# One-hot rows of a routing-weight table: made in bfloat16 by the vector engine, eight tokens at a time

## The chip, the core and the metric

The kernel runs on one core of a Trainium2 chip. The core has a matrix engine (TensorE, in the profile PE for its products and PEld for its weight loads), a vector engine (VectorE, DVE), a scalar engine (ScalarE, ACT), GpSimd (POOL) and SyncE (SP), which here only issues transfers. Every engine works through its own list of instructions in a fixed order and waits on semaphores for the others. The metric is the device time of one execution in microseconds (us), the median of the runs.

## The reference

Two layers of a diffusion transformer: 512 latent tokens and 256 context tokens of 1024 channels. Each layer has three mixers, a merge and, at its end, a retrieval of experts with product keys. Only the last matters here, cut to its core (per token block):

```python
s1, i1 = lax.top_k(s[:, :, 0], 16)            # 8 heads, two halves of 128 keys each
s2, i2 = lax.top_k(s[:, :, 1], 16)
cand_s = (s1[..., :, None] + s2[..., None, :])
top_s, pos = lax.top_k(cand_s, 16)            # the 16 best pairs: expert i1*128 + i2
g = softmax(top_s)
act = gelu(einsum('td,thkd->thk', t, u_tab[idx]))
return einsum('thk,thkd->td', g * act, v_tab[idx])
```

There are 128 x 128 = 16384 experts and each token uses 8 x 16 = 128 of them.

## The kernel before

Everything is done in float32 precision. Large products split each operand into a high part with few significant bits and an exact rest (`split`, lines 96 to 109: ACT makes the high part on line 102, DVE or POOL subtracts it on line 109) and add three products (`mm3`, lines 113 to 115). "alt" as an engine means that DVE and POOL take the subtraction in turns.

The experts are evaluated in two ways. A few token blocks of 128 tokens gather the rows of their experts from DRAM, one expert row of every token at a time (`step`, line 838 on POOL asks for the rows, lines 857 and 866 on DVE use them); these steps are spread over the whole program. For the other latent blocks, four in layer 0 and three in layer 1 (`NDBS`), all 16384 experts are evaluated densely, 128 experts (a chunk) at a time: `dense_u` makes gelu(u h) for a chunk, 24 products, tile du, then gS; `dense_v` multiplies gS by the routing weights of the chunk and multiplies by v (tiles da and d).

The routing weights must stand as a dense table [i1][i2][token] in DRAM before `dense_v` can start. `gtable` makes it, one block of 128 tokens at a time, for seven blocks or 896 tokens in all. A block is transposed on PE so that the 128 (head, rank) slots lie on the partitions (i1, i2 and the weight g of each slot; line 896), and ACT copies these to the tile sT (lines 899, 900, the second negated). Then, for each token, two matrices of 128 slots x 128 columns are made: oa, with a one where the column is i1, and ob, with g where the column is i2. One product per token of ob and oa (line 919, tile px) sums over the slots and gives the token's 128 x 128 table. In detail, for four tokens at a time:

- oa: one DVE instruction, a comparison of 512 float32 elements (line 908).
- ob: one instruction per token, and the engine depends on the token: the letters of `OB = ("PADD", "AADD")` are POOL, ACT and DVE. So of eight tokens POOL makes one and DVE four, each in one instruction (line 916), and ACT three, each in two instructions (lines 913, 914).
- four products on PE in float32; the trace records two matrix instructions for each (1792 for 896 tokens).
- one ACT copy of 512 elements from PSUM to the staging tile stg (line 920). After 16 tokens SP stores stg in DRAM (line 921), and `gtable` yields.

oa and ob have three buffers each (`OBB`), px has two PSUM banks.

The work around it: `layer` interleaves four generators, among them `routing` (norm, `route1`, then `route2` for each block), `table` (`gtable` for each dense block once its `route2` is done) and `fill`, which runs `dense_u` ahead of the table. `route2` picks the 16 best pairs on DVE (lines 684 to 688) and looks up their keys: a DVE comparison of 2048 bfloat16 elements into a tile oh (line 773, its first operand a broadcast with an innermost step of 0), a POOL product in place (line 776), a DVE sum (line 777). The pool gives this tile, tag "oh", one buffer. `fill` keeps the results of its chunks in buffers: `NGSS = (16, 30)` of them in SBUF for layers 0 and 1, besides 40 chunks per layer that go to DRAM. The remaining chunks of u are made in the dense stage, between the v parts. The order in which each engine finally runs its instructions is fixed when the program is built, by a planner with its own durations; products of du stand between products of px in it.

Of the kernel before, what the change touches and what calls it, by code (L numbers as in the profile page):

```python
# [10 lines left out]
F32 = mybir.dt.float32  # L11
F32R = mybir.dt.float32r
# [9 lines left out]
P = 128  # L22
# [8 lines left out]
CAND = 112         # pairs of best keys that can be among the 16 best  # L31
NK = 128
NDBS = (4, 3)      # latent token blocks whose experts are evaluated densely, per layer
OBB = 3            # buffers of the one-hot rows
XB = 2             # steps of adaLN before each of the first two norms
XA = (4, 4)        # and before the loads of each of the inputs
GP = ("px", "px")  # PSUM tags of the routing-weight table
BRE = "dve"        # engines: split of the mixers' results,
YS = "dve"         # split of the merged mixers,
ADDE = "dve"       # sums of the mixers  # L40
OB = ("PADD", "AADD") # engines of the one-hot rows of four tokens, in turns
PQB = (2, 2)       # buffers of the query weights of the routing: split, and as loaded
PQC = None         # and of the context
US = ("alt", "alt") # engine that splits the expert tables beside the routing, per layer
GT = 16            # tokens per group of the routing-weight table
NCG = 8            # chunks of experts per read of that table
TILE = 1800        # ns to load a weight tile
STEPS = ((1700, 1700, 1700), (1700, 1700, 1700)) # ns between two steps of the gathered experts: mixers, dense experts
LAG = 3            # steps from a gathered product to its sum
NGSS = (16, 30)    # chunks of experts by which u runs ahead of v, per layer  # L50
SPILL = ((40, 3), (40, 3)) # chunks whose u part goes to DRAM early, one in so many, per layer
FILL = (1.0, 1.3)  # steps of u and adaLN per step of the routing
LEAD = 2           # of which so many after the routing
ADA = 6            # adaLN column groups of the next layer beside its predecessor's routing
WBUFS = ((3, 2), (3, 4)) # buffers of weight tiles: split, and as loaded, per layer
FB = (1, 2)        # buffers of the Fourier matrices, per layer
PE2 = ("alt", "dve") # engines that split the weights of the projections, per layer
PE3 = ("dve", "dve") # and of q, k and v
ME = ("alt", "pool") # engines that split the weights of the merge beside the attention, per layer
CR = 1.75          # steps of the routing of the context per step of the last merge  # L60
CR2 = 1            # and per step of the routing of the latents
GATES = (0.5, 0.6) # steps of the gates per step of the Fourier and chunk mixers, per layer
ATT = (3, 1)       # steps of the merge per step of the attention, per layer
AN = (0.1, 0.2)    # and per step of the second norm
AD = (0.25, 0.3)   # steps of adaLN per step of the Fourier and chunk mixers, per layer

# tile numbers of the packed projection weights
# [6 lines left out]
PBANKS = {"ps": 4, "px": 2, "tl": 1, "fl": 1}     # PSUM banks of the projections  # L74
RBANKS = {"ps": 3, "px": 2, "tl": 2, "fl": 1}     # and from the attention on


class Ker:
# [19 lines left out]
    def split(self, H, L, src, h="act", l="dve"):  # L98
        """src = H + L, H with float32r's significant bits, L the exact rest."""
        nc = self.nc  # L100
        if h == "act":
            nc.scalar.activation(H, src, AF.Copy)  # L102
        else:
            nc.vector.tensor_copy(H, src)
        if l == "alt":          # both in turns
            self.turn = not self.turn
            l = "dve" if self.turn else "pool"
        e = nc.vector if l == "dve" else nc.gpsimd
        e.tensor_tensor(L, src, H.bitcast(F32), op=ALU.subtract)  # L109
# [8 lines left out]
    def mm3pair(self, out, qH, qL, kH, kL, h, qs):  # L118
        """the two halves of a head's 128 rows, on the two row tiles of the array."""
# [6 lines left out]
    def hilo(self, src, l="dve", own=None):  # L126
        """a [128, 1024] weight tile from DRAM, in two float32r parts; own: (pool, buffers of the parts, and as loaded)."""
# [17 lines left out]
    def interleave(*threads, until=None):  # L145
        """emits generators in turns, each (generator, steps per turn); all, or until one ends."""
# [19 lines left out]
    def rstd(self, tmp, r, v, scale, shape, tag, bufs=1, eps=None):  # L166
        """r = (v * scale + eps) ** -0.5: Newton steps from the guess that halves the exponent."""
# [16 lines left out]
    def setup(self):  # L184
# [9 lines left out]
        self.csil = cp.tile([P, KD, 4], F32R, name="csilr")      # high parts of both vectors, then low parts  # L194
# [13 lines left out]
    def setup_rest(self):  # L208
# [3 lines left out]
        self.iota = cp.tile([P, P], F32, name="iota")  # L212
        nc.sync.dma_start(self.iota, a["iota"])
        self.iota16 = cp.tile([P, TOPK], BF16, name="iota16")
        nc.vector.tensor_copy(self.iota16, self.iota[:, :TOPK])
        for l, v in enumerate(self.lay):
# [11 lines left out]
            nc.vector.tensor_tensor(v["lam"], e[:, 1:2], e[:, 0:1], op=ALU.subtract)     # minus lambda  # L228
# [4 lines left out]
    def ada(self, l, ccs, pool=None, e="dve", tag="tl"):  # L233
        nc = self.nc
        sm, mod = self.lay[l]["sm"], self.lay[l]["mod"]
        for cc in ccs:
# [19 lines left out]
            if cc in (3, 9):          # norm gain times (1 + scale)  # L256
# [7 lines left out]
    def sumsq(self, tmp, S, k, src, tag="nt", bufs=2):  # L264
        """adds the squares of channel block k to S."""
# [8 lines left out]
    def rms(self, tmp, S, scale, T, ps=None):  # L274
        """1 / rms of the columns of S (squares, summed over the partitions), on every partition, in PSUM."""
        return self.spread(self.rmsd(tmp, S, scale, T, ps), T, ps)

    def rmsd(self, tmp, S, scale, T, ps=None, eps=None):
        """its first half: the values as diagonal matrices of 128 columns each."""
# [17 lines left out]
    def stat(self, tmp, r, T, load):  # L297
        """r = 1 / rms of the columns."""
# [4 lines left out]
    def norm(self, tmp, l, xd, T, which, si, outs, r=None, x=None, *_):  # L303
        """outs(k) -> (H, L) for channel block k; xd: [128, 8, T] in DRAM; r: 1 / rms where known; x: xd in SBUF."""
# [23 lines left out]
    def projT(self, l, n, ss, e="pool", tag=None, own=None):  # L328
        """(h @ W)^T of each stream: 128 columns on the partitions."""
# [10 lines left out]
    def projN(self, l, n, ss, e="pool"):  # L340
        """h @ W for 512 columns of each stream, tokens on the partitions."""
# [14 lines left out]
    def qknorm(self, tmp, accs, g, rope, oH, oL):  # L356
        """accs: PSUM [128 tokens, 512]; oH, oL: [128 (m, dim), head, token]."""
# [58 lines left out]
    def softmax(self, tmp, l, h, q0, qH, qL, T, klat, kctx, ze):  # L416
        """the two softmaxes of a head for 256 queries and their difference, per 128 queries; ze: EPS for the norm."""
# [13 lines left out]
        for qb in range(2):  # L431
# [18 lines left out]
            # the difference, times the sum of the first softmax, which the norm of the result takes out again  # L450
# [941 lines left out]
```

## Time and profile before

| | us |
|---|---|
| median of 3 runs | 5004.7 (4994.27 to 5005.57) |
| span of the profiled execution | 4993.1 |
| PE busy | 4532.1 |
| DVE busy | 3535.6 |
| POOL busy | 2083.6 |
| ACT busy | 1995.8 |

The span runs from the first to the last instruction of one profiled execution. It is 1.2 us below the fastest of the runs and 11.6 us below their median. Busy time counts the time in which an engine had an instruction in work; for DVE and POOL that includes time in which the instruction was held up, as some rows below show. The table stage of layer 0 lies at 1280 to 1680 us and that of layer 1 at 3840 to 4130 us; what comes before is the mixers and most of the routing, and what comes after each is the dense stage.

### The profile page before, as it was taken

The numbers are of one execution on the slowest core, as the hardware profiler recorded it, in microseconds if no ns is written. First come the engines' busy times: TensorE is split into PE (matmuls) and PEld (weight loads), VectorE is DVE, ScalarE is ACT, GpSimd is POOL, SyncE is SP. The second block draws the span as 40 slices with busy tenths as digits, with TensorE's granted clock in tenths as the row PEclk, the third lists the DMA queues.
The fourth block names the chain that finished last, engine by engine and source line by source line (L and its number), as shares of the span: only waits on it lengthen the run. The fifth ranks groups of instructions, "written<-read, shape, count | busy, mean of one in ns | idle before, by whom it ended". The sixth has DMA issues, their size and how long they took to land.

```text
span 4993.1 us, 64879 instructions
## 1 busy us (share of the span) xinstructions
PE 4532.1 (91%) x23117; PEld 3852.4 (77%) x23117; DVE 3535.6 (71%) x6922; ACT 1995.8 (40%) x3274; POOL 2083.6 (42%) x1262
## 2 busy tenths in 40 slices
PE   7999989788788899999999989989897899999998
PEld 4887778667566688877778767767687788999998
DVE  6335585977998677766767875457559986777787
ACT  4433443232678522222222233334333783333332
POOL 2111013345656565655556421111326665555531
PEclk8999999899999999999999989999898999999999
DMA  4532345566566889988889876233535668888886
GB/s 167 178 115 65 98 128 180 165 191 197 193 232 226 290 288 318 320 281 270 280 284 304 310 256 217 94 102 110 163 97 180 214 245 293 294 293 301 300 286 232
DMA packets 447364, 1092.82 MB, mean 219 GB/s; under 512 B 37056, under 2 KB 193600, under 8 KB 439872
## 3 DMA queue, kind: packets, MB, share of 16 engines
q1 hardware_dynamic: 336448, 685.97, 42.4%
q0 software_dynamic: 110592, 402.70, 23.7%
q8 instruction: 182, 2.98, 0.2%
q14 instruction: 142, 1.16, 0.1%
HBM read 970.04 MB, written 118.49 MB: 218 GB/s over the span
## 4 chain that ended last, share of the span: by engine, by line
PE 55%; DVE 17%; issue 8%; DMA 8%; POOL 5%; ACT 3%; SPq 0%; POOLq 0%; ACTq 0%; DVEq 0%
PE du L113 6%; PE du L115 5%; PE du L114 5%; PE da L114 5%; PE da L113 5%; PE da L115 5%; PE ps L114 3%; PE ps L113 3%; PE ps L115 3%; DVE row L857 2%; POOL row L838 2%; DMA row<-in_u_dram,idxc 2%; PE px L919 2%; POOL wL L109 2%; DVE wL L109 2%
## 5 line engine op out<-in xcount | busy, mean ns | idle before, releaser
L109 POOL TENSOR_TENSOR wL<-wraw,wH 128x1024 fp32r<-128x1024 f32 x307 | 761.7, 2482 | 1197.1 <-ACT wH L102 1066.9
L102 ACT ACTIVATE wH<-wraw 128x1024 fp32r<-128x1024 f32 x556 | 586.8, 1058 | 1231.5 <-PE du L114 337.2
L113 PE MATMUL du<-dH,wH 128*128 128x512 f32 (+1 forms) x2048 | 779.9, 381 | 64.4 <-DVE da L980 46.3
L115 PE MATMUL du<-dH,wL 128*128 128x512 f32 (+1 forms) x2048 | 773.2, 378 | 49.0 <-POOL wL L109 27.4
L114 PE MATMUL du<-dL,wH 128*128 128x512 f32 (+1 forms) x2048 | 770.2, 376 | 4.1 <-DVE dL L325 4.1
L114 PE MATMUL da<-AL,vH 128*128 128x512 f32 (+1 forms) x1792 | 650.5, 363 | 3.0 <-DVE AL L109 2.9
L113 PE MATMUL da<-AH,vH 128*128 128x512 f32 (+1 forms) x1792 | 646.4, 363 | 6.0 <-ACT AH L102 6.0
L115 PE MATMUL da<-AH,vL 128*128 128x512 f32 (+1 forms) x1792 | 649.5, 362 | 0.0
L857 DVE SCALAR_TENSOR_TENSOR row<-row,hn 128x1024 f32<-128x1024 f32 x384 | 526.9, 1392 | 99.4 <-DMA row<-in_u_dram,idxc 83.6
L102 ACT ACTIVATE vH<-vr 128x1024 fp32r<-128x1024 f32 x256 | 271.7, 1062 | 772.5 <-PE da L114 559.3
L109 DVE TENSOR_TENSOR wL<-wraw,wH 128x1024 fp32r<-128x1024 f32 x249 | 336.9, 1355 | 330.7 <-ACT wH L102 316.7
L866 DVE SCALAR_TENSOR_TENSOR acc<-row,dots,acc 128x1024 f32<-128x1024 f32 x381 | 502.9, 1320 | 10.8 <-DMA row<-in_v_dram,idxc 6.9
L838 POOL DMA_INDIRECT row<-in_v_dram,idxc x256 | 336.1, 1313 | 400.5 <-DVE acc L866 325.3
L113 PEld LDWEIGHTS du<-dH,wH 128*128 128x128 f32 x2048 | 399.5, 195 | 121.1 <-DVE da L980 56.6
L115 PEld LDWEIGHTS du<-dH,wL 128*128 128x128 f32 x2048 | 398.9, 195 | 99.5 <-POOL wL L109 31.9
L838 POOL DMA_INDIRECT row<-in_u_dram,idxc x256 | 340.7, 1331 | 300.3 <-DVE row L857 203.7
L114 PEld LDWEIGHTS du<-dL,wH 128*128 128x128 f32 x2048 | 399.4, 195 | 44.5 <-DVE dL L325 5.4
L980 DVE TENSOR_TENSOR da<-d,da 128x512 f32<-128x512 f32 (+1 forms) x254 | 158.2, 623 | 328.1 <-PE d L115 327.7
L113 PEld LDWEIGHTS da<-AH,vH 128*128 128x128 f32 x1792 | 337.2, 188 | 42.2 <-ACT AH L102 7.2
L114 PEld LDWEIGHTS da<-AL,vH 128*128 128x128 f32 x1792 | 337.3, 188 | 41.1 <-DVE AL L109 6.0
L115 PEld LDWEIGHTS da<-AH,vL 128*128 128x128 f32 x1792 | 337.3, 188 | 35.1
L109 DVE TENSOR_TENSOR vL<-vr,vH 128x1024 fp32r<-128x1024 f32 x256 | 326.1, 1274 | 47.4 <-ACT vH L102 45.4
(389 smaller groups left out, 9543.7 us busy)
## 6 DMA issues: line engine op xcount, KB each, us to landing
wraw<-in_uT_dram SPq DMA_DIRECT2D x256, 512.0 KB, 4.5
vr<-in_v_dram SPq DMA_DIRECT2D x256, 512.0 KB, 6.5
wraw<-in_wt_dram SPq DMA_DIRECT2D x204, 512.0 KB, 3.8
gd<-stg SPq DMA_DIRECT2D x56, 1024.0 KB, 5.2
wraw<-in_wada_dram SPq DMA_DIRECT2D x96, 512.0 KB, 4.2
gt<-gd SPq DMA_DIRECT2D x16, 2048.0 KB, 16.8
gt<-gd SPq DMA_DIRECT2D x16, 1536.0 KB, 12.9
gatex<-g SPq DMA_DIRECT2D x48, 256.0 KB, 2.4
```

The lines of the kernel that those rows point to most:

```text
L102: nc.scalar.activation(H, src, AF.Copy)
L109: e.tensor_tensor(L, src, H.bitcast(F32), op=ALU.subtract)
L113: nc.tensor.matmul(out, aH, bH, start=start, stop=False)
L114: nc.tensor.matmul(out, aH, bL, start=False, stop=False)
L115: nc.tensor.matmul(out, aL, bH, start=False, stop=stop)
L838: nc.gpsimd.indirect_dma_start(out=row, out_offset=None, in_=self.a[f"{job['tab']}{job['l']}"], in_offset=bass.IndirectOffsetOnAxis(ap=r[" ...
L857: nc.vector.scalar_tensor_tensor(row, row, 1.0, job["hn"], op0=ALU.mult, op1=ALU.mult, accum_out=dots[:, j:j + 1])
L866: nc.vector.scalar_tensor_tensor(job["acc"], row, dots[:, j:j + 1], job["acc"], op0=ALU.mult, op1=ALU.add)
L919: nc.tensor.matmul(gp[:, j * P:(j + 1) * P], ob[:, j, :], oa[:, j, :], start=True, stop=True)
L980: add = nc.vector.tensor_tensor(acc7, s[:, :TD], acc7, op=ALU.add)
```

## The change

`gtable` is written anew; the comments and named constants go (no effect), and one number changes elsewhere: `NGSS` from (16, 30) to (16, 28), so two chunks of u fewer run ahead of the table in layer 1.

- The column numbers (`iota`) are kept in bfloat16 (exact up to 128) as `iotab`. Per block ACT writes i1 and i2 in bfloat16, each value twice side by side (ix), and g as a sum of three bfloat16 parts, again each twice (gx): ACT rounds, DVE subtracts what was rounded off from the rest, twice.
- Eight tokens at a time DVE makes oa (i1 equals column), oh (i2 equals column) and the three products of oh with the parts of g (ob). These are five two-operand instructions of 1024 bfloat16 elements each. All operands are laid out in pairs: the innermost dimension has two elements with step 1, also for the broadcast one. ACT and POOL make no one-hot rows any more.
- PE makes three bfloat16 products per token, summed in PSUM, in place of one in float32.
- The ACT copy to stg and the store are as before. oa and ob have two buffers; oh has one, under the tag "oh" that `route2` uses too, in the same pool.

```diff
-OB = ("PADD", "AADD")
-NGSS = (16, 30)
+NGSS = (16, 28)
-        sT = tmp.tile([P, 5, P], F32, tag="sT", name=self.nm("sT"), bufs=2)
-        nc.scalar.activation(sT[:, :3, :], tp3, AF.Copy)
-        nc.scalar.activation(sT[:, 3:, :], tp3[:, 1:, :], AF.Copy, scale=-1.0)
+        sh = [P, 2, P, 2]
+        ix = tmp.tile(sh, BF16, tag="ix", name=self.nm("ix"), bufs=2)
+        nc.scalar.activation(ix, tp3[:, :2, :].unsqueeze(3).to_broadcast(sh), AF.Copy)
+        gx = tmp.tile([P, 3, P, 2], BF16, tag="gx", name=self.nm("gx"), bufs=2)
+        rest = tmp.tile([P, 2, P], F32, tag="gr", name=self.nm("gr"), bufs=1)
+        left = tp3[:, 2, :]
+        for i in range(3):
+            nc.scalar.activation(gx[:, i], left.unsqueeze(2).to_broadcast([P, P, 2]), AF.Copy)
+            if i < 2:
+                nc.vector.tensor_tensor(rest[:, i, :], left, gx[:, i, :, 0], op=ALU.subtract)
+                left = rest[:, i, :]
+        NT = 8
+        sh = [P, NT, P // 2, 2]
+        io = self.iotab.rearrange("p (a b) -> p a b", b=2).unsqueeze(1).to_broadcast(sh)
+        pairs = lambda x: x.rearrange("p t (a b) -> p t a b", b=2)
...
-            for t in range(0, GT, 4):
-                sh = [P, 4, NK]
-                nc.vector.tensor_tensor(oa, sT[:, 0, c:c + 4].unsqueeze(2).to_broadcast(sh), io, op=ALU.is_equal)
-                for j, e in enumerate(OB[t // 4 % 2]):
-                    if e == "A":
-                        nc.scalar.activation(ob[:, j, :], self.iota, AF.Abs, bias=sT[:, 3, c + j:c + j + 1], scale=1.0)
-                        nc.scalar.activation(ob[:, j, :], ob[:, j, :], AF.Relu, bias=g, scale=sT[:, 4, c + j:c + j + 1])
-                    else:
-                        (nc.vector if e == "D" else nc.gpsimd).tensor_scalar(ob[:, j, :], self.iota, i2, g, op0=ALU.is_equal, op1=ALU.mult)
-                for j in range(4):
-                    nc.tensor.matmul(gp[:, j * P:(j + 1) * P], ob[:, j, :], oa[:, j, :], start=True, stop=True)
+            for t0 in range(0, GT, NT):
+                wide = lambda x: x[:, g0 + t0:g0 + t0 + NT, :].unsqueeze(2).to_broadcast(sh)
+                oa = tmp.tile([P, NT, P], BF16, tag="oa", name=self.nm("oa"), bufs=2)
+                nc.vector.tensor_tensor(pairs(oa), wide(ix[:, 0]), io, op=ALU.is_equal)
+                oh = tmp.tile([P, NT, P], BF16, tag="oh", name=self.nm("oh"), bufs=1)
+                nc.vector.tensor_tensor(pairs(oh), wide(ix[:, 1]), io, op=ALU.is_equal)
+                ob = tmp.tile([P, 3, NT, P], BF16, tag="ob", name=self.nm("ob"), bufs=2)
+                for i in range(3):
+                    nc.vector.tensor_tensor(pairs(ob[:, i]), pairs(oh), wide(gx[:, i]), op=ALU.mult)
+                for t in range(0, NT, 4):
+                    for j in range(4):
+                        for i in range(3):
+                            nc.tensor.matmul(gp[:, j * P:(j + 1) * P], ob[:, i, t + j, :], oa[:, t + j, :], start=(i == 0), stop=(i == 2))
```

## Rows read from the trace of the kernel before

**Rows 1.** The page: busy time, share of the span and instructions of each engine
```profile
span 4993.1 us, 64879 instructions
PE 4532.1 (91%) x23117; PEld 3852.4 (77%) x23117; DVE 3535.6 (71%) x6922; ACT 1995.8 (40%) x3274; POOL 2083.6 (42%) x1262
```

**Rows 2.** Busy time by stretch; each line starts with start:end and length in us
```profile
core 0: us, PE busy (x) PEld busy (x) DVE busy (x) ACT busy (x) POOL busy (x), PEclk, DMA share, GB/s
1280.00:1580.00 300.00, 247.94 (x1343) 199.30 (x1342) 287.31 (x637) 230.60 (x448) 183.86 (x109) 0.94 0.65 219
1580.00:1680.00 100.00, 93.44 (x521) 73.86 (x521) 77.11 (x139) 81.84 (x158) 57.91 (x38) 1.00 0.72 243
3840.00:4000.00 160.00, 127.74 (x765) 117.94 (x764) 153.34 (x318) 121.18 (x240) 95.98 (x56) 0.93 0.58 199
4000.00:4130.00 130.00, 122.18 (x777) 111.78 (x777) 101.95 (x190) 111.05 (x221) 77.99 (x52) 0.99 0.72 252
```

**Rows 3.** Line 908 alone, by the same stretches: DVE busy and instructions
```profile
1280.00:1580.00 300.00, 77.10 (x96) 0.94 0.65 219
1580.00:1680.00 100.00, 26.81 (x32) 1.00 0.72 243
3840.00:4000.00 160.00, 48.84 (x51) 0.93 0.58 199
4000.00:4130.00 130.00, 33.81 (x46) 0.99 0.72 252
sum 690.00, DVE 186.56; mean DVE 46.64
```

**Rows 4.** Lines 919, 908, 913, 914, 916: instructions, ns min/median/max, first and last start
```profile
L919 PE MATMUL px<-oa,ob x1792: 270/275/581, 1282.7 to 4127.0; 128*128 128x128 f32 x200
L908 DVE TENSOR_TENSOR oa<-sT,iota x224: 666/681/4537, 1281.4 to 4122.1; 128x512 f32<-128x512 f32 x112
L913 ACT ACTIVATE ob<-iota,sT x336: 355/394/462, 1280.1 to 4124.7; 128x128 f32<-128x128 f32 x168
L914 ACT ACTIVATE ob<-ob,sT x336: 446/480/554, 1280.7 to 4125.8; 128x128 f32<-128x128 f32 x168
L916 DVE TENSOR_SCALAR ob<-iota,sT x448: 324/338/4111, 1282.0 to 4122.9; 128x128 f32<-128x128 f32 x150
```

**Rows 5.** DVE in order of time (start us, us), table work undisturbed
```profile
1389.55 0.67 DVE L908 TENSOR_TENSOR oa<-sT,iota 128x512 f32<-128x512 f32 x1
1390.15 0.58 DVE L916 TENSOR_SCALAR ob<-iota,sT 128x128 f32<-128x128 f32 x2
1390.66 0.67 DVE L908 TENSOR_TENSOR oa<-sT,iota 128x512 f32<-128x512 f32 x1
```

**Rows 6.** Lines 773 and 109 on DVE: instructions, ns min/median/max
```profile
L773 DVE TENSOR_TENSOR oh<-pb,iota x20: 2266/2280/2292, 944.3 to 3976.4; 128x2048 bf16<-128x2048 bf16 x20
L109 DVE TENSOR_TENSOR wL<-wraw,wH x249: 1198/1225/5075, 7.4 to 4151.2; 128x1024 fp32r<-128x1024 f32 x125
```

**Rows 7.** DVE and POOL in order of time, around one lookup of keys
```profile
1437.54 4.08 POOL L776 TENSOR_TENSOR oh<-oh,pIF 128x2048 bf16<-128x2048 bf16 x1 [5.08 <-DVE oh L773]
1437.93 4.24 DVE L908 TENSOR_TENSOR oa<-sT,iota 128x512 f32<-128x512 f32 x1
...
1349.10 2.27 DVE L773 TENSOR_TENSOR oh<-pb,iota 128x2048 bf16<-128x2048 bf16 x1
1351.90 4.34 DVE L916 TENSOR_SCALAR ob<-iota,sT 128x128 f32<-128x128 f32 x2
1366.13 2.27 DVE L777 TENSOR_REDUCE i2x<-oh 128x128 f32<-128x2048 bf16 x1
```

**Rows 8.** Sum lines: DVE and POOL busy with line 916, and DVE with line 777
```profile
sum 690.00, DVE 201.38 POOL 150.89; mean DVE 50.34 POOL 37.72
sum 690.00, DVE 22.74; mean DVE 5.68
```

**Rows 9.** PE in order of time: products of px, then of du with 384 columns
```profile
1392.26 1.82 PE L919 MATMUL px<-oa,ob 128*128 128x128 f32 x14
...
4299.82 0.33 PE L113 MATMUL du<-dH,wH 128*128 128x384 f32 x1
4299.99 0.33 PE L114 MATMUL du<-dL,wH 128*128 128x384 f32 x1
```

**Rows 10.** What ended PE's idle time before line 919: us, times
```profile
  ACT ob L914: 54.0, 96
  POOL ob L916: 31.7, 19
  DVE oa L908: 27.8, 16
  DVE ob L916: 23.1, 12
  ACT ob L913: 12.6, 9
```

**Rows 11.** DVE groups, 1280 to 1680 us: busy us, mean ns, idle before, releaser
```profile
L908 DVE TENSOR_TENSOR oa<-sT,iota 128x512 f32<-128x512 f32 x128 | 103.9, 812 | 12.5 <-PE px L919 12.4
L109 DVE TENSOR_TENSOR wL<-wraw,wH 128x1024 fp32r<-128x1024 f32 x23 | 30.9, 1345 | 18.8 <-ACT wH L102 18.7
L780 DVE TENSOR_TENSOR gx<-pTS 128x128 f32<-128x128 f32 x3 | 0.8, 274 | 0.0
```

**Rows 12.** All engines by stretch: the dense stage of layer 1
```profile
4250.00:4500.00 250.00, 244.93 (x1395) 242.77 (x1395) 186.52 (x257) 88.11 (x118) 144.20 (x89) 0.99 0.87 292
```

More of the change, by code (lines that the diff above doesn't have):

```diff
@@ L33 @@
 NDBS = (4, 3)
-OBB = 3
 XB = 2
@@ L211, in setup_rest @@
         nc.vector.tensor_copy(self.identr, self.ident)
[L212 to L215, printed above, removed]
+        iota = cp.tile([P, P], F32, name="iota")
+        nc.sync.dma_start(iota, a["iota"])
+        self.iotab = cp.tile([P, P], BF16, name="iotab")
+        nc.vector.tensor_copy(self.iotab, iota)
+        self.iota16 = self.iotab[:, :TOPK]
         for l, v in enumerate(self.lay):
@@ L901, in gtable @@
+        io = self.iotab.rearrange("p (a b) -> p a b", b=2).unsqueeze(1).to_broadcast(sh)
+        pairs = lambda x: x.rearrange("p t (a b) -> p t a b", b=2)
         for g0 in range(0, P, GT):
             stg = tmp.tile([P, NK, GT], F32, tag="stg", name=self.nm("stg"), bufs=2)
-            for t in range(0, GT, 4):
-                sh = [P, 4, NK]
-                io = self.iota.unsqueeze(1).to_broadcast(sh)
-                c = g0 + t
-                oa = tmp.tile(sh, F32, tag="oa", name=self.nm("oa"), bufs=OBB)
-                nc.vector.tensor_tensor(oa, sT[:, 0, c:c + 4].unsqueeze(2).to_broadcast(sh), io, op=ALU.is_equal)
-                ob = tmp.tile(sh, F32, tag="ob", name=self.nm("ob"), bufs=OBB)
-                for j, e in enumerate(OB[t // 4 % 2]):
-                    i1, i2, g = (sT[:, i, c + j:c + j + 1] for i in (0, 1, 2))
-                    if e == "A":
-                        nc.scalar.activation(ob[:, j, :], self.iota, AF.Abs, bias=sT[:, 3, c + j:c + j + 1], scale=1.0)
-                        nc.scalar.activation(ob[:, j, :], ob[:, j, :], AF.Relu, bias=g, scale=sT[:, 4, c + j:c + j + 1])
-                    else:
-                        (nc.vector if e == "D" else nc.gpsimd).tensor_scalar(ob[:, j, :], self.iota, i2, g, op0=ALU.is_equal, op1=ALU.mult)
-                gp = self.ps(GP[t // 4 % len(GP)])
-                for j in range(4):
-                    nc.tensor.matmul(gp[:, j * P:(j + 1) * P], ob[:, j, :], oa[:, j, :], start=True, stop=True)
-                nc.scalar.activation(stg[:, :, t:t + 4].rearrange("p a t -> p t a"), gp.rearrange("p (t a) -> p t a", t=4), AF.Copy)
@@ new lines, in gtable @@
+            for t0 in range(0, GT, NT):
[8 more added lines that the diff above has]
+                for t in range(0, NT, 4):
+                    gp = self.ps(GP[t // 4 % len(GP)])
+                    for j in range(4):
+                        for i in range(3):
+                            nc.tensor.matmul(gp[:, j * P:(j + 1) * P], ob[:, i, t + j, :], oa[:, t + j, :], start=(i == 0), stop=(i == 2))
+                    nc.scalar.activation(stg[:, :, t0 + t:t0 + t + 4].rearrange("p a t -> p t a"), gp.rearrange("p (t a) -> p t a", t=4), AF.Copy)
```

## The prediction

> **What bounds the kernel now.** I read the page first: PE is busy 91% of the span and DVE 71% [rows 1]. That share is a mean over stages, so it doesn't say what bounds the stage that is changed. The second view cuts out the two table stages, and each again at the point where routing work ends (1580 us in layer 0, 4000 us in layer 1) and only the table and the chunks of u are left [rows 2]. In the first part of each stage DVE is busy 287.3 of 300 us and 153.3 of 160 us, 96% both times, while PE has 248 of 300 and 128 of 160 us. In the second part PE is the fuller one, 93.4 of 100 and 122.2 of 130 us, with DVE at 77.1 and 102.0 us and ACT at 81.8 and 111.1. So the routing part is bound by DVE, and the tail by PE with ACT close behind.
>
> The third view says how much of it is table work. Line 908 has one instruction for four tokens, so its counts give the tokens of each stretch in fours: 96, 32, 51 and 46, 225 in all (one lies across a border; there are 224) [rows 3]. Of the engines that make the one-hot rows, PE waits longest for ACT: 54.0 + 12.6 us before line 919, against 27.8 + 23.1 us for DVE and 31.7 us for POOL [rows 10]. These waits are real, but they count only where PE is the bound; where DVE is at 96% a shorter wait for ACT lets DVE reach its own end no sooner.
>
> The fourth view is on what a busy DVE does. Two of its table instructions took 4.24 and 4.34 us where their medians are 0.68 and, for two, 0.68 us: they start while a POOL product of two SBUF operands is in work and end with it [rows 4, 7]. So part of DVE's busy time is standing still beside POOL.
>
> **The change, part by part.**
>
> ACT's one-hot work goes: 336 x 0.394 + 336 x 0.480 = 294 us [rows 4]. POOL's goes: 150.9 us [rows 8]. Neither engine is the bound of the first parts, so this gives nothing there by itself. In the tails ACT is at 82% and 85% and gives way. ACT gets four small copies per block in place of two; I take it as nothing, since it has just lost ten times as much.
>
> DVE. Undisturbed, four tokens cost it one comparison and two rows of ob, and the next comparison starts 1390.66 - 1389.55 = 1.11 us later [rows 5]; of this the comparison takes 0.60 us from start to start. After the change eight tokens take five instructions of 1024 bfloat16 elements with two operands. No row of this trace has such an instruction in a faster mode. The bounds are the row with 512 elements per instruction, 0.60 us from start to start, if two elements go through at a time, and the 1024-element row, 1.225 us long, if one does [rows 5, 6]. I take 0.60: an operand of 1024 such elements has as many bytes as one of 512 float32 elements, and the new layout puts every element beside a partner. Then eight tokens cost 3.0 us against 2.22, so four cost 0.39 us more. Over the stretches that is 96 x 0.39 = 37, 32 x 0.39 = 12, 51 x 0.39 = 20 and 46 x 0.39 = 18 us: 87 us more DVE work, not less. To this come two subtractions per block, 14 x 0.274 = 4 us by a two-operand instruction of that size [rows 11].
>
> The one bfloat16 comparison that the trace has, line 773, takes 2.28 us for 2048 elements, against 1.225 us for 1024 float32 elements on line 109 [rows 6]: 1.03 ns an element either way, no faster for the smaller type. Its first operand repeats a single element; taken alone, it speaks for the slow bound, which is the third rival.
> [...]
>
> DVE has idle time that could take the 91 us: 12.7, 22.9, 6.7 and 28.1 us in the four stretches [rows 2], of which 12.5 us before line 908 in layer 0 waited for PE to free a buffer and 18.8 us before line 109 waited for ACT [rows 11]; both should shrink. In the first parts, at 96% now, I let the new 37 and 20 us lengthen the stage by between 57 us (nothing absorbed) and 57 - 19 = 38 us (all of the idle time used). In the tails DVE needs 77.1 + 12 = 89 of 100 and 102.0 + 18 = 120 of 130 us; if it can be 96% full there as in the first parts, they end at 93 and 125 us at the earliest, so the tails give back up to 7 and 5 us, if PE lets them.
>
> PE. Now two passes per product, 14 passes in 1.82 us: 0.13 us each, 0.26 us a token [rows 9]. Then three bfloat16 passes a token, of which the trace has none. The bounds: a float32 pass, 0.13 us, gives 0.39 us a token; a third of a 384-column product, 0.17 us from start to start, gives 0.057 us for 128 columns and 0.17 us a token [rows 9]. I take 0.07 us, nearer to the lower end as bfloat16 needs no second pass, 0.21 us a token. In the tails, with 128 and 184 tokens, that is 6 and 9 us less for PE, about what DVE lets through: -10 us for both tails. The upper bound would make it +17 and +24 us.
>
> The stall beside POOL. The new instructions all have two SBUF operands, as line 908 has. The time lost now is 186.6 - 224 x 0.60 = 52 us at most in line 908 [rows 3, 5] and 201.4 - 448 x 0.255 = 87 us at most in line 916 [rows 8, 5]; by the medians, which count overlapping starts, 34 and 50 us [rows 4]. POOL's products of lines 109 and 776, beside which they stand, stay. If the new ones lose at line 908's rate, 34 us per 134 us of work, 336 us lose 85 us: as much as the 84 us now. So nothing is added or taken.
> [...]
>
> The shared buffer. `route2` holds its one buffer "oh" from line 773 to the end of line 777, 1349.10 to 1368.4 us in one case, and table work on both ob and oa ran in between [rows 7]; now oh of the table can't. Line 777 runs 10 times in the stretches (22.7 us by 2.27) [rows 8]. DVE stands still beside line 776 anyway, so I take 0; if each cost another 4.1 us, it is +41 us.
>
> NGSS. Two chunks of u move from the tail of layer 1 into the dense stage, where PE is busy 245 of 250 us [rows 12]: 2 x 24 x 0.173 = 8 us later there [rows 9], and up to 8 us earlier in the tail, where DVE's 125 us now stand in the way. I take +4, bounds 0 and 8.
>
> **The sum.** First parts +48 (38 to 57), subtractions +4, tails -10, NGSS +4: +46 us. The span of 4993.1 us becomes 5039; the runs lie 1.2 to 12.5 us above the span, so I put the difference on the median: 5004.7 + 46 = 5051 us. What this forecast's own bounds make: from 38 - 12 = +26 to 57 + 4 + 41 + 8 = +110 us, that is 5031 to 5115.
>
> **The rivals.**
>
> *Faster: DVE's occupancy is standing still, and PE sets the end.* If the new instructions don't stand still beside POOL, the 84 us go and DVE's work grows by only 91 - 84 = 7 us. Then PE, relieved of waits on ACT and POOL of 54.0 + 12.6 + 31.7 = 98 us [rows 10], decides; about half of it comes through: -45 us, 4960. It decides once stalls fall by more than 50 us. For it: line 916, which goes, stands still more often for its work than line 908. Against it: the 4.24 us row is line 908's own.
>
> *No change.* The idle 70 us of DVE in the stretches take nearly all of the 91 us, and PE's shorter products (896 x 0.05 = 45 us) give the rest: 5005. Against it: the routing parts have 19 us idle for 57.
>
> *Much slower: one element per cycle.* The pair layout isn't taken in the fast mode. Then eight tokens cost 5 x 1.14 = 5.7 us against 2.22, 112 x 3.5 = 390 us more, less the 70 idle: +320 us, 5325. For it: the only bfloat16 comparison of the trace. Against it: that one has no pairs.
>
> *Slower by PE.* At 0.13 us a pass the tails grow by 41 us instead of falling by 10: 5102; it lies within the forecast's bounds.
>
> **How the numbers follow.** Forecast with its PE variant 0.60, much slower 0.08, no change 0.13, faster 0.19. A measurement of this kernel can tell about 0.3%, 15 us, from no change. Slower by more than that: 0.60 of the forecast (all of it is above 5020) and 0.08, less a little for a forecast that absorbs more: 0.65. Within 15 us: 0.15. Faster: 0.20. The range leaves out the much slower case and the larger half of the faster one: 4980 to 5115; the forecast's own is 5031 to 5115.
>
> **What would show it.** Line by line in the profile after: the five instructions at 0.60 us from start to start (1.2 would be the third rival); DVE at 96% or more through both stages, tails included; the stages some 30 and 15 us longer; PE's waits before px on DVE and no longer on ACT or POOL; DVE instructions of the table of 2 to 4 us beside POOL's products as now (if they are gone, the first rival); bfloat16 passes at 0.06 to 0.08 us. The prediction is wrong if table stages get shorter with DVE full: then the added work must have replaced lost time that I have counted as staying.

## The result, and the profile after

The changed kernel takes 5032.98 us (median of 4 runs, 5031.47 to 5036.71); the kernel before, beside it on the same chip, 4999.49 us (4 runs, 4993.52 to 5005.57). The ratio is 1.0062, with a 95% interval from 1.005 to 1.0074: 33 us slower, where the forecast had 46. The span of the profiled execution goes from 4993.1 to 5034.9 us.

The page of the kernel after, busy time, share of the span and instructions of each engine, stands against [rows 1]:

```profile
span 5034.9 us, 65266 instructions
PE 4517.9 (90%) x24013; PEld 3806.0 (76%) x24013; DVE 3613.6 (72%) x6823; ACT 1799.5 (36%) x2616; POOL 1956.1 (39%) x1151
```

ACT is relieved by 196 us and POOL by 128, DVE is busy 78 us longer. Where this matters is seen when the two table stages are cut out, from DVE's first one-hot rows to the last product of px. First the kernel before (each line: start:end, length, busy us and instructions by engine, granted TensorE clock, DMA share, GB/s):

```profile
1280.00:1673.00 393.00, 334.38 (x1831) 267.33 (x1830) 360.81 (x770) 309.80 (x602) 238.13 (x144) 0.96 0.66 224
3848.00:4127.00 279.00, 241.15 (x1488) 221.32 (x1489) 247.29 (x483) 225.93 (x448) 170.46 (x106) 0.95 0.64 221
sum 672.00, PE 575.52 PEld 488.65 DVE 608.11 ACT 535.73 POOL 408.60; mean PE 287.76 PEld 244.32 DVE 304.05 ACT 267.86 POOL 204.30
```

and the same view of the kernel after:

```profile
1281.00:1705.00 424.00, 331.06 (x2361) 238.64 (x2360) 402.72 (x717) 197.60 (x225) 175.12 (x81) 0.87 0.61 209
3875.00:4178.00 303.00, 237.82 (x1907) 208.66 (x1908) 289.22 (x441) 146.28 (x174) 109.44 (x58) 0.88 0.60 206
sum 727.00, PE 568.87 PEld 447.30 DVE 691.94 ACT 343.87 POOL 284.56; mean PE 284.44 PEld 223.65 DVE 345.97 ACT 171.94 POOL 142.28
```

The stages are 31 and 24 us longer. The length of a stage is DVE's busy time plus its idle time in it: 608.1 + 63.9 us before, 691.9 + 35.1 after. So DVE is busy 84 us longer, and 29 us of that went into time in which it had been idle. DVE is now busy 95% of both stages, PE 78% against 86% before.

What a table instruction costs now is seen in DVE's order of time (start us, us, engine, line):

```profile
1546.39 0.68 DVE L919 TENSOR_TENSOR oa<-ix,iotab 128x1024 bf16<-128x1024 bf16 x1
1546.99 0.68 DVE L921 TENSOR_TENSOR oh<-ix,iotab 128x1024 bf16<-128x1024 bf16 x1
...
1552.30 2.66 DVE L919 TENSOR_TENSOR oa<-ix,iotab 128x1024 bf16<-128x1024 bf16 x1
```

1546.99 - 1546.39 = 0.60 us from start to start for 1024 bfloat16 elements, what line 908 took for 512 float32 elements [rows 5]. The third row is one that stands still: it took 2.66 us, and its partner on POOL is this:

```profile
1552.03 2.37 POOL L107 TENSOR_TENSOR wL<-wraw,wH 128x1024 fp32r<-128x1024 f32 x1
```

The view by line of the kernel after (ns min/median/max, first and last start), to be read beside [rows 4]:

```profile
L919 DVE TENSOR_TENSOR oa<-ix,iotab x112: 662/682/4978, 1281.8 to 4168.7; 128x1024 bf16<-128x1024 bf16 x112
L921 DVE TENSOR_TENSOR oh<-ix,iotab x112: 661/680/2892, 1282.6 to 4172.3; 128x1024 bf16<-128x1024 bf16 x112
L924 DVE TENSOR_TENSOR ob<-oh,gx x336: 664/680/3251, 1283.4 to 4175.2; 128x1024 bf16<-128x1024 bf16 x168
L929 PE MATMUL px<-oa,ob x2688: 216/219/330, 1284.1 to 4177.4; 128*128 128x128 bf16 x192
```

And what ended PE's idle time before px in the kernel after (us, times), the view of [rows 10]:

```profile
  DVE ob L924: 197.1, 209
  issue: 35.0, 145
  ACT stg L930: 11.7, 27
```

Waits for the one-hot rows of ACT and POOL, 54.0, 12.6 and 31.7 us before, are gone, and the wait for those of DVE is nearly four times as long as both of its rows together (27.8 + 23.1).

### The profile page after: what moved, and what is told of

It reads as the page before. It is cut to its first block, busy times and chain, and to the rows that moved or that the text cites. A ratio compares the mean times of both kernels' runs of the same rounds, so it can differ in the third digit from the quotient of the medians.

```text
span 5034.9 us, 65266 instructions
## 1 busy us (share of the span) xinstructions
PE 4517.9 (90%) x24013; PEld 3806.0 (76%) x24013; DVE 3613.6 (72%) x6823; ACT 1799.5 (36%) x2616; POOL 1956.1 (39%) x1151
## 4 chain that ended last, share of the span: by engine, by line
PE 54%; DVE 20%; DMA 8%; issue 6%; POOL 4%; ACT 2%; SPq 0%; POOLq 0%; DVEq 0%; ACTq 0%
PE du L111 6%; PE du L113 6%; PE du L112 5%; PE da L112 5%; PE da L113 5%; PE da L111 5%; PE ps L112 3%; PE ps L113 3%; PE ps L111 3%; DVE row L856 3%; DVE ob L924 3%; POOL wL L107 2%; DMA row<-in_u_dram,idxc 2%; DVE wL L107 2%; PE px L111 1%
## 5 line engine op out<-in xcount | busy, mean ns | idle before, releaser
L107 POOL TENSOR_TENSOR wL<-wraw,wH 128x1024 fp32r<-128x1024 f32 x308 | 790.7, 2568 | 1243.9 <-ACT wH L100 1130.4
L113 PE MATMUL du<-dH,wL 128*128 128x512 f32 (+1 forms) x2048 | 783.6, 383 | 70.8 <-POOL wL L107 41.2
L113 PEld LDWEIGHTS da<-AH,vL 128*128 128x128 f32 x1792 | 337.6, 188 | 35.1
```

The costliest lines, as they stand in the source:

```text
L113: nc.tensor.matmul(out, aL, bH, start=False, stop=stop)
```

## The experiments

The theory: in the changed kernel the stage lasts as long as DVE has work in it, so the time follows DVE's instructions and nothing else of the change. Its rivals: that PE's third pass, or the half again as many matrix instructions of px, set the time; that the shared buffer or the moved chunks of u cost the 33 us; that the rate of 0.60 us doesn't come from the pairs. In all diffs "+" is the edit, and lines are those of the kernel after unless the text says otherwise. Ratios are to the kernel before, run on the same chip in turns.

**Fewer parts of g.** The table loses a part of its precision here: with two parts the weights have about 16 significant bits, with one 8.

```
-                for i in range(3):            # DVE products, and likewise the passes on PE
+                for i in range(2):            # e2: range(1)
```

> The changed kernel with two of the three parts of the weight g (the smallest part is left out, so the table holds g to 16 bits only): per eight tokens four DVE instructions instead of five, two PE passes per token instead of three. Theory (the table stages are bound by DVE's work, so the time follows it): 112 x 0.60 = 67 us less DVE work than the changed kernel and 20 us more than before; with DVE full from end to end that gives 4970 to 4990 us, at most as far down as PE allows. Rival (the loss comes from something else that the change brought: the two chunks fewer ahead, the shared buffer, another order of the instructions): most of the loss stays, 5015 us or more.

> The changed kernel with one of the three parts of g (g in bfloat16 only): three DVE instructions per eight tokens, one PE pass per token. Theory: another 67 us less DVE work, 47 us less than before; PE is near its bound by then (91 to 94% in the tails of before), so the second step gives less than the first: 4930 to 4960 us. Rival (order, buffer, chunks): it stays above 4990.

Two parts: 4961.3 us, ratio 0.9922 (0.9896 to 0.9948). One part: 4909.88 us, 0.9817 (0.9796 to 0.9839). Each part is 112 DVE instructions of 0.60 us, 67 us of work. The first that goes takes 72 us with it, the second 51; both times lie below the ranges that were expected. The sum lines of the two stages, with two parts and with one:

```profile
sum 650.00, PE 503.74 PEld 395.50 DVE 627.57 ACT 338.87 POOL 261.66; mean PE 251.87 PEld 197.75 DVE 313.79 ACT 169.43 POOL 130.83
sum 590.00, PE 433.45 PEld 345.48 DVE 558.69 ACT 332.34 POOL 266.80; mean PE 216.72 PEld 172.74 DVE 279.35 ACT 166.17 POOL 133.40
```

DVE falls by 64 and 69 us, the stages by 77 and 60, and DVE's idle time stays small (22 and 31 us). A part takes PE's work away as well, though, so this alone doesn't tell DVE from PE.

**Only the passes.** DVE still makes all three products; PE uses only the first, so the table lacks the two lower parts of g.

```
-                        for i in range(3):
+                        for i in range(1):    # line 928, the passes on PE alone
```

> The changed kernel with all five DVE instructions, but only the first of the three PE passes per token (the two smaller parts are made and not used). PE has 896 x 2 passes less, at 0.055 to 0.07 us 100 to 125 us of PE work. Theory (DVE sets the end): 0 to -10 us, 5023 to 5033. Rival (PE's table work is on the path): -40 us or more, 4990.

5041.38 us, ratio 1.0079 (1.0057 to 1.01): no faster than with three passes (1.005 to 1.0074); the median is above the 5023 to 5033 expected, but the two intervals overlap. PE has 1792 matrix instructions and 90 us of busy time less in the stages, and the stages are as long as without this edit, 729 and 727 us:

```profile
1276.00:1707.00 431.00, 281.96 (x1320) 201.68 (x1318) 412.50 (x713) 194.47 (x224) 160.21 (x80) 0.78 0.59 205
3870.00:4168.00 298.00, 196.80 (x1104) 176.97 (x1105) 279.55 (x436) 139.67 (x168) 104.73 (x56) 0.77 0.60 205
sum 729.00, PE 478.76 PEld 378.65 DVE 692.05 ACT 334.15 POOL 264.93; mean PE 239.38 PEld 189.32 DVE 346.02 ACT 167.07 POOL 132.47
```

DVE's 692.05 us are those of the changed kernel to 0.1 us. So PE's passes alone are worth nothing here, and the 72 and 51 us above need DVE's part of the cut. That they would come as fully with all of PE's passes kept isn't shown: no version takes products from DVE alone.

**Chunks of u alone.** The kernel before with the number that the change sets elsewhere.

```
-NGSS = (16, 30)
+NGSS = (16, 28)
```

> The kernel before with NGSS (16, 28) instead of (16, 30), nothing else. My step put +4 us on it, bounds 0 and 8: 5000 to 5008 beside about 5000 of before. Rival (the two chunks fewer carry a good part of the 33 us): +15 us or more.

5003.32 us, ratio 1.0008 (0.9996 to 1.002): between 2 us less and 10 us more, as expected. The bulk of the 33 us doesn't come from it.

**No pairs.** The broadcast operand repeats one element, as in line 773 of the kernel before.

```
-                wide = lambda x: x[:, g0 + t0:g0 + t0 + NT, :].unsqueeze(2).to_broadcast(sh)
+                wide = lambda x: x[:, g0 + t0:g0 + t0 + NT, 0].unsqueeze(2).unsqueeze(3).to_broadcast(sh)
```

> The changed kernel, with the broadcast operand of the five instructions read as a single element repeated (innermost step 0) instead of pairs. [...] If the pairs don't matter: 5033.

5320.58 us (one run; 5004.01 before). The same types, sizes and counts, only the innermost step of one operand differs:

```profile
L919 DVE TENSOR_TENSOR oa<-ix,iotab x112: 1197/1215/5130, 1282.8 to 4447.2; 128x1024 bf16<-128x1024 bf16 x112
...
1305.08 1.21 DVE L919 TENSOR_TENSOR oa<-ix,iotab 128x1024 bf16<-128x1024 bf16 x1
1306.21 1.21 DVE L921 TENSOR_TENSOR oh<-ix,iotab 128x1024 bf16<-128x1024 bf16 x1
```

An instruction is 1.21 us long against 0.68, and the next starts 1.13 us later against 0.60. That is the case of the prediction's third rival, which forecast 5325. So without the pairs the change costs 317 us, by this one run.

**An own buffer for oh.** The shared buffer goes; one chunk of u is given up in layer 1 to make room for it.

```
-NGSS = (16, 28)
+NGSS = (16, 27)
-                oh = tmp.tile([P, NT, P], BF16, tag="oh", name=self.nm("oh"), bufs=1)
+                oh = tmp.tile([P, NT, P], BF16, tag="ohg", name=self.nm("oh"), bufs=1)
```

> The changed kernel with a buffer of its own for the table's oh (tag ohg); NGSS goes to (16, 27) to make room for it. My step put 0 on the shared buffer, bound 41 us. Theory (DVE sets the end, and it stands still beside the POOL product in either case): 5025 to 5035. Rival (the shared buffer blocks the table while keys are looked up): 4995 to 5010.

5042.72 us, ratio 1.0087 (1.0055 to 1.0119); the interval of the changed kernel overlaps with it, and the median is above the 5025 to 5035 expected. DVE is busy 684.3 us of stages of 732 us. An own buffer gives back nothing that can be seen; one chunk of u less is in this run as well, but in the run on chunks alone two of them are worth 10 us at most.

**The same move without bfloat16.** The kernel before, all one-hot rows on DVE in float32: this does the one half of the change (off ACT and POOL) without the other; the passes on PE, the buffers and the chunks of u stay as before too.

```
-OB = ("PADD", "AADD")
+OB = ("DDDD", "DDDD")
```

> The kernel before with all rows of ob made by DVE (OB = DDDD twice), in float32 as before: ACT and POOL are freed as in the change, and DVE has 448 x 0.255 = 114 us more work, against 92 us in the change. If freeing ACT and POOL gives back what the change got beside its added DVE work (about 58 us), 5000 + 114 - 58 = about 5055 us. If what it got comes from the bfloat16 products on PE or from fewer instructions, 5100 us or more.

5056.09 us, ratio 1.0108 (1.0076 to 1.014), as expected. The stages:

```profile
sum 730.00, PE 585.09 PEld 505.87 DVE 716.84 ACT 346.67 POOL 263.98; mean PE 292.54 PEld 252.94 DVE 358.42 ACT 173.34 POOL 131.99
```

So the change is two steps of opposite sign. Taking the rows off ACT and POOL costs 52 us by the medians; making them in bfloat16, five instructions for eight tokens in place of ten, with all that comes with it, gives back 19 by the medians, each less that of its kernel before (52.1 - 33.5), or 23 by the ratios (0.0046 x 5000). In work, eight tokens are 2 x 0.60 + 8 x 0.255 = 3.24 us in float32 [rows 5] and 5 x 0.60 = 3.0 in bfloat16: 112 x 0.24 = 27 us, and DVE's busy time differs by 716.8 - 691.9 = 25.

What ended DVE's idle time tells where the 29 us of absorbed work went. Before, in the stage of layer 0 and then in that of layer 1 (engine and line that waits, line waited for: us, times, longest):

```profile
DVE wL L109 <- ACT wH L102: 15.3, 6, 4.7
DVE oa L908 <- PE px L919: 12.4, 12, 3.1
...
DVE oa L908 <- PE px L919: 15.7, 16, 4.0
DVE wL L109 <- ACT wH L102: 14.8, 6, 7.3
```

and after, layer 0, then layer 1:

```profile
DVE oa L919 <- PE px L929: 9.4, 6, 3.4
...
DVE gr L908 <- ACT gx L906: 2.3, 2, 1.5
DVE wL L107 <- ACT wH L100: 1.7, 1, 1.7
...
DVE oa L919 <- PE px L929: 10.7, 11, 2.6
DVE gr L908 <- ACT gx L906: 3.0, 2, 1.8
```

The split of a table of u is made by ACT (high part) and then DVE (rest). With ACT busy 80% DVE waited 30.1 us for the high part, with ACT at 47% it waits 1.7. A new wait of 5.3 us for ACT's rounding of g (the tiles gx and gr) takes some of that back. The wait for PE to free a buffer of oa falls only from 28.1 to 20.1 us. It doesn't come from the number of PE's passes: with one pass in place of three it is 24.4 us (10.4 + 14.0). The kernel before with all rows on DVE, with three buffers in place of two, shows none of it; that the number of buffers is the reason wasn't tested.

**Splits off POOL.** If a DVE instruction stands still for as long as a POOL product runs, a product that takes POOL 2.4 us should be cheaper on DVE itself, at 1.22, however full DVE is. First in the changed kernel, then in the kernel before.

```
-US = ("alt", "alt")
+US = ("dve", "dve")
```

> The changed kernel with all splits of the expert tables beside the routing on DVE (US = dve) instead of DVE and POOL in turns. Theory of the standing still (a POOL product of 2.4 us holds DVE for most of its length, and the same split on DVE takes 1.22 us): each split moved costs DVE 1.2 us of work and gives back about 2 us, so some 45 splits give -20 to -40 us: 4995 to 5015. If DVE's standing still doesn't come from POOL's splits: 45 x 1.2 = +55 us, 5085.

> The kernel before with all splits of the expert tables beside the routing on DVE (US = dve), nothing else. In the changed kernel this step gave about 20 us: DVE's standing still fell by 58 us in the two stretches and its work rose by 41. If DVE's standing still was as much of a loss in the kernel before: 4980 to 4990 us. If ACT and PE hold the kernel before back just as much (its DVE idles 68 us in the stretches): no change, 4995 to 5005.

In the changed kernel: 5013.75 us, ratio 1.0019 (1.0002 to 1.0036), some 20 us faster than without the edit, within what was expected. In the kernel before: 4992.73 us, 0.9981 (0.9966 to 0.9996), 7 us, between the two cases that were expected. The lines of the split alone, in the two stages of the changed kernel, without the edit (DVE 38 instructions, POOL 38) and with it (69 and 7):

```profile
sum 727.00, DVE 56.39 POOL 122.94; mean DVE 28.19 POOL 61.47
sum 705.00, DVE 87.51 POOL 25.37; mean DVE 43.75 POOL 12.69
```

and the sums of lines 919 and 924, without and with:

```profile
sum 727.00, DVE 114.67; mean DVE 57.33
sum 705.00, DVE 97.61; mean DVE 48.81
...
sum 727.00, DVE 232.14; mean DVE 116.07
sum 705.00, DVE 217.58; mean DVE 108.79
```

DVE takes on 31 us of splits and loses 17 + 15 us on these two lines and 9 on line 921 (84.91 to 75.78): 41. With what other lines lose, its busy time falls by 16 us (691.9 to 675.5) while it does 31 splits more. POOL's splits are longer beside the full DVE too: one takes 122.94 / 38 = 3.2 us on average here, 9.10 us in the longest (from 1315.67 us), against 2.4 in the median of the whole program and 97.96 / 39 = 2.5 on average in the stages of the kernel before.

In the kernel before, DVE's busy time in the stages falls by more, 36 us (608.1 to 572.0), and the stages are no shorter for it, 672 us in both profiles. The sum, and two of DVE's waits in the stage of layer 1:

```profile
sum 672.00, PE 585.47 PEld 498.01 DVE 571.97 ACT 544.66 POOL 375.04; mean PE 292.73 PEld 249.00 DVE 285.99 ACT 272.33 POOL 187.52
...
DVE i1x L777 <- POOL oh L776: 11.6, 2, 6.0
DVE i2x L777 <- POOL oh L776: 9.6, 2, 4.8
```

DVE's idle time grows by the same 36 us, from 63.9 to 100.0. With 16.7 us in layer 0 it now waits 37.9 us for POOL's product of the lookup of keys, for which it didn't wait before; the waits for ACT's high parts (29.9 us) and for PE (23.1 us) are still there. So in the kernel before, with ACT and POOL loaded too, less busy time of DVE was no shorter stage. (The execution profiled here is 9.5 us above the median of its runs.)

**A third of the products back on ACT.** If DVE is the bound and ACT has room, ACT should make the third part of ob (128 instructions of 128 elements per block). It multiplies by the second remainder itself, in float32, as a scale per slot. oh has two buffers of its own and the remainder two, and to make room for them three chunks of u go (`NGSS` is (16, 25)); of the edit this is the core:

```
-                for i in range(3):            # DVE products
+                for i in range(2):
...
+                for t in range(NT):
+                    c = g0 + t0 + t
+                    nc.scalar.activation(ob[:, 2, t, :], oh[:, t, :], AF.Copy, scale=rest[:, 1, c:c + 1])
```

> The changed kernel with the third product of ob on ACT, one instruction per token (same numbers, all three parts): DVE has 112 x 0.60 = 67 us less, ACT 896 x 0.36 = 323 us more, on an engine that is busy 45% of the time in the stages of the changed kernel. oh has two buffers of its own, NGSS is (16, 25) to make room. Theory (DVE sets the end, ACT has room): close to the run with two parts, 4961, plus what PE now waits for ACT: 4970 to 4995. If ACT's waits come back as in the kernel before: 5000 to 5015.

5021.22 us, ratio 1.0031 (1.0015 to 1.0047): faster than the changed kernel by 12 to 15 us, where 38 to 63 were expected, and above the 5015 that were named for the case that ACT's waits come back. The stages:

```profile
sum 701.00, PE 569.83 PEld 447.46 DVE 611.16 ACT 579.19 POOL 282.41; mean PE 284.92 PEld 223.73 DVE 305.58 ACT 289.59 POOL 141.20
L927 ACT ACTIVATE ob<-oh,gr x896: 351/393/473, 1286.0 to 4155.6; 128x128 bf16<-128x128 bf16 x180
```

DVE's busy time falls by 81 us, 67 of them the product given away, but ACT is at 83% again and DVE's idle time goes up to 701 - 611.2 = 90 us. The stages are 26 us shorter, and not all of that reaches the end: 43 matrix instructions of u more than in the changed kernel (1622 against 1579) stand in the dense stage of layer 1. The waits of DVE in the stage of layer 0:

```profile
DVE oa L919 <- PE px L932: 11.9, 7, 5.0
DVE wL L107 <- ACT wH L100: 9.8, 7, 3.0
DVE oh L921 <- ACT ob L927: 8.7, 8, 2.5
```

The wait for the high part of the splits is back, and a new one beside it: the buffers of oh, which ACT reads to the end. So DVE's full stage in the changed kernel rests on ACT being free; with ACT loaded as before, DVE's idle time is 90 us instead of 35. What the three chunks less have to do with it isn't told apart here.

**Both together.** The last edit with splits off POOL, and two parts with splits off POOL (the weights with about 16 bits).

> The same with the splits beside the routing on DVE too (US = dve). If the two steps add up, 20 us below the run before: 4950 to 4975.

> Two of the three parts of g (g to 16 bits) and all splits beside the routing on DVE: the two steps that helped most, together. With three parts the second step gave about 20 us in the changed kernel. Theory (stage length is DVE's work plus its standing still plus its idle time, and ACT and POOL have room here): the steps add up, 4961 - 20 = 4935 to 4950. If PE or ACT takes over as the bound: 4961 or little less.

The first: 4998.22 us, 0.9994 (0.998 to 1.0008), 23 us below the version with the splits on both engines, the step that was expected, but not the 4950 to 4975, and not to be told from the kernel before. The second: 4936.57 us, 0.987 (0.9841 to 0.9899), within what was expected. The steps add up: 72 us for a part and 19 for the splits from 5033 would be 4942. It is the fastest here that is of any use if 16 bits of the weights are enough; with all bits, no version of the bfloat16 rows beat the kernel before.

## Why the prediction was right, step by step

**The bound.** Right for the changed kernel. While ACT and POOL are free, DVE's busy time and the stages fall together (by 64 and 77 us, 69 and 60, 16 and 22), and PE's work can be cut by 90 us without effect (the one-pass version). It doesn't hold in every experiment: with ACT loaded again DVE's busy time fell by 81 us and the stages by 26, and in the kernel before, with the splits off POOL, it fell by 36 us and the stages by nothing. So the 96% that the prediction read told rightly that added work of DVE lengthens the stage; they don't tell that less of it would shorten it. Of the signs that it named, the 96% came out as 95, and the stages grew by 31 and 24 us instead of some 30 and 15.

**What leaves ACT and POOL.** The forecast gave it nothing by itself and let DVE's idle time shrink: of 91 us of new work 49 were to be absorbed, 42 to lengthen the stages. Measured: 84 us of work, 29 absorbed, 55 longer. The direction and the agent were right: of the 29 us, waits for ACT give 23 (28.4 less for the high parts, 5.3 more for the rounding of g) and the wait for px 8, while other waits grew by 2. The size was not, and where it failed is seen when the stages are cut at the end of the routing, now at 1612 and 4084 us (DVE is the third figure behind the length):

```profile
1281.00:1612.00 331.00, 249.72 (x1722) 180.69 (x1720) 313.66 (x592) 148.93 (x169) 143.45 (x63) 0.85 0.59 203
1612.00:1705.00 93.00, 81.33 (x639) 57.95 (x640) 89.06 (x126) 48.67 (x56) 31.67 (x19) 0.94 0.67 232
3875.00:4084.00 209.00, 159.73 (x1236) 140.85 (x1237) 200.90 (x314) 96.39 (x114) 80.75 (x38) 0.86 0.57 196
4084.00:4178.00 94.00, 78.08 (x672) 67.81 (x672) 88.32 (x128) 49.89 (x60) 28.69 (x20) 0.91 0.67 230
```

In the tails DVE is idle 3.9 + 5.7 = 9.6 us, as good as the 4 + 5 that the forecast left there (93 - 89 and 125 - 120). In the first parts it let the 19 us of idle time shrink to 10, and they are 17.3 + 8.1 = 25.4: 14.9 us of waits for px are in it, and 4.1 for the rounding of g, on which the forecast put nothing.

**DVE's rate.** Right to the digit: 0.60 us from start to start, 224 x 0.39 = 87 us of added table work forecast, 84 us more busy time measured with the subtractions and all standing still (of which less is left, see below). The rival on the other side was the row of line 773, and the version without pairs is near that line's rate: 1.13 us from start to start for 1024 elements, where line 773 took 2.28 us for 2048 [rows 6]. With pairs it is 0.60. That the pairs make the difference is shown by these two versions; why they do isn't shown by any run.

**Tails.** The forecast let PE's cheaper passes shorten the second parts of the stages by 10 us. The passes are cheaper than taken. Each has one matrix instruction (2688 for 3 x 896), where a float32 product has two [rows 4], and 20 of them in one stretch of the kernel after,

```profile
1547.79 1.29 PE L929 MATMUL px<-oa,ob 128*128 128x128 bf16 x20
```

are at most 0.065 us each, against 0.07 taken and 0.13 for a float32 pass [rows 9]. But it isn't PE's passes that fill the tails, as the one-pass version shows; they fill because DVE's idle time there goes, as said above. The mis-sized part of the sum is what DVE's idle time would take: 29 us in place of 49. DVE's busy time grew by 84 us in place of 91, so the stages, which were to grow by 42 us, grew by 55.

**Standing still beside POOL.** Taken as unchanged, 84 us by the medians. In the kernel after the same reckoning gives 114.7 - 112 x 0.682 = 38 us on line 919, 9 on line 921 and 4 on line 924, 51 in all: 33 less. (It is low for the lines whose records overlap. By the sum of single durations line 924 lost 21 us and line 916 of the kernel before 68, which makes 102 and 68: 34 less.) It isn't gone: the lookup of keys takes DVE 27.1 us instead of 22.8, line 856 121.2 us for 179 records instead of 111.4 for 173, and the splits on DVE 56.4 us for 38 instead of 48.0 for 37. Less the work of what is more in number (three pairs of records at 1.3 us, a split at 1.2), that is 4 + 6 + 7 = 17 us of the 33. So the faster rival, which needed more than 50 us of it to go, had its mechanism partly right and its condition unmet. What holds DVE up beside such a product isn't shown by any run. The 2.66 us row began 0.27 us after the 2.37 us split and ended 0.56 us behind it, and the version with the splits on DVE is 20 us faster.

**The shared buffer and the chunks of u.** Taken as 0 and +4; measured as nothing that can be told, and between -2 and +10. The two chunks didn't move as the prediction had it: with the smaller number alone the kernel before has 1623 matrix instructions of u in the dense stage of layer 1, against 1624 without.

**The rest.** Outside the two stages the profile after is 13 us shorter (4307.9 against 4321.1 us), where the forecast had +4. By the spans, +55 - 13 = +42, near the forecast of +46, because two errors nearly cancel: that it comes so near is luck. The medians differ by 33; the span before lies near the fastest of its runs, the one after is that of the slowest of its four. Of the 13, 9 are in the dense stage of layer 1, 866.1 us before and 856.9 after:

```profile
4127.00:4993.10 866.10, 830.99 (x4707) 820.31 (x4705) 638.06 (x818) 293.32 (x392) 415.25 (x266) 0.99 0.85 286
4178.00:5034.90 856.90, 821.10 (x4659) 811.97 (x4657) 635.63 (x814) 290.37 (x389) 416.81 (x267) 0.98 0.84 287
```

There are 48 matrix instructions fewer in it, 45 of them of u (two chunks have 48): a longer table stage takes in more of u (749 products of du against 715), which fits that part of what the stage loses is given back behind it, in spite of the smaller NGSS. But this can't be the whole: the kernel before with all rows on DVE has the same stretch at 860.9 us with no product of u fewer, and the stretch from the table of layer 0 to that of layer 1 differs by up to 24 us between single profiles of these versions, without an order that I can see. What makes up the 13 us stays open.

**The range.** The sum for its upper end, +110 us, has one term of 41 us where the prediction has two (the shared buffer and PE's slow passes); with both it would be +151. The lower end leaves out the 4 us of subtractions. Neither end was reached.

**What would have made it wrong.** Table stages that are shorter with DVE full were named as the sign; they came only where DVE's work or its standing still was cut.

## What to carry to other kernels

Where one engine fills a stage, count what a change adds to that engine first, from start to start: a change that took 324 us of busy time off two less busy engines (196 and 128) made the kernel 33 us slower, since it added 84 us to the third. The idle time of the full engine is what such a change may win; look up whom it waits for, since at most that part (here 30 us of waiting for ACT, 23 net) comes back. The other way round is no rule: work taken off the full engine shortened the stages by as much only while the other engines had room. And ask of every GpSimd product beside a full DVE whether DVE wouldn't do it in less time than it stands still for (here 1.22 us for a split, where a row of 0.68 us took 2.66 beside one on POOL).

## What the runs showed of the hardware

- A split of 1024 elements cost less on the fuller engine than on the emptier one: 1.22 us on DVE (busy 95% of the stages after) against 2.4 us and more on POOL (39%), and beside one of 2.37 us a DVE row of 0.68 us took 2.66. Moving 31 of them to DVE made DVE's busy time 16 us shorter. In the kernel before the same edit made it 36 us shorter, and yet the stages stayed at 672 us and the time fell by 7 us: DVE's waits took the place of its work, 37.9 us of them for POOL.
- A pass of 128 bfloat16 columns with its weight load took at most 0.065 us from start to start, half of what the same reckoning gives for a float32 pass (0.13 us); three of them were a product of full weights in 0.19 us against 0.26.
- The granted clock of TensorE in the two stages fell from 0.96 and 0.95 of full speed to 0.87 and 0.88 while PE was busy 78% instead of 86%, and to 0.78 and 0.77 in the one-pass version (66%). The one-pass version has the lowest clock and stages as long as with three passes (729 and 727 us), so the lower clock costs no time that can be seen here.
